# One step of a hybrid RWKV-7 / Conformer backbone on one core: a lane scheduler that stays longer in dense products, and a late modulation with stationary weights

## The chip, the core and the metric

The kernel runs on one core of a Trainium2 chip. The metric is the time of one execution on the device in microseconds (us), lower is better. Engines are named as the profile names them: PE is TensorE's products and PEld its weight loads, DVE is VectorE, ACT ScalarE, POOL GpSimd, SP the queue that issues the DMAs.

## What is computed

One trunk layer for 128 context and 512 latent tokens, D = 1024, in float32. Cut to what matters here:

```python
mod = silu(cond) @ ada_w + ada_b                      # 6 x 1024 columns: shift, scale, gate, twice
xn  = rmsnorm(x) * (1 + sc1) + sh1
rkv, glu_in, gates = split(xn @ w_in)
y_r = rwkv_branch(xn, rkv, s0_f, s0_b)                # two scans, 8 heads x 64, per-step recurrence
y_c = conv_branch(glu_in)                             # depthwise conv, LayerNorm, silu, projection
x   = x + g1 * ((sigmoid(gate_r) * y_r + sigmoid(gate_c) * y_c) @ w_o)
x   = x + g2 * (relu((rmsnorm(x) * (1 + sc2) + sh2) @ mlp_w1) ** 2 @ mlp_w2)
```

The modulation is needed in two portions: its first 16 blocks of 128 columns before the input projection, the other 32 (`for c in range(16, 48)`) only for block 1's gate, block 2 and the second norm.

## The kernel before

All activations stand feature-major: 640 tokens along the free axis in two halves of 320, 128 features on the partitions. A **dense** product is one 128x128 block of weights against 320 tokens. Each operand is split into a high and a low part in `float32r`, and three products (`mm3`) make one float32 result. Their weights come from HBM as `wr`, are split by ACT (`wh`) and DVE (`wl`), and are used in the order of `todo`. Everything else on PE is plain float32, which the trace shows as two instructions for each product: the scan's, the Gram matrices', the norms' and the late modulation's. These are called **small** products below.

The program has three stages. The first computes the early modulation, the first norm and the low-rank inputs. In the second, generators called **lanes** (`solve`, `scan`, `side`, `prep`, `lora2_all`, `ada_all`, `out_branch`, `conv_all`, `splitter`) carry the RWKV branch, the convolution and the late modulation, while `fill` supplies dense products between their steps. The third runs the output projection and the MLP, nearly all dense.

In the second stage the order of PE, DVE and ACT is fixed when the program is built, by a planner in the kernel with its own clock `now[0]` and its own costs. Each turn of the main loop calls `pick`, which returns the first lane that is due (`l[0] <= now[0]`); lanes are sorted by urgency (`URGENT`, a small number is urgent). A lane that would put products on PE (`l[1]` is None) is taken only when `hungry()` is false. Otherwise `more()` places the next dense product. `hungry()` is true while the planner believes that PE's clock has dropped, or while `credit` is below zero; each dense product raises `credit`, up to `CREDIT`, and time lowers it. What stands earlier in an engine's order is waited for: a PE product whose input is late stops all behind it.

The late modulation is the lane `ada_all`, urgency 4. For each block of 128 columns, `adl_load` fetches two halves of the weights (256 KB each) into one buffer `adl`, so that the second half's DMA can't start before the products of the first are done. `ada` then makes 2 x 4 products with the conditioning vectors `csb` stationary (32 columns) and the weights moving (128 columns), spread over four column groups of the array (`tile_position=(0, g)`). ACT copies the result out (`ade`), one product with `sel` folds the four groups, and ACT adds the bias into `mod`.

The end of the second stage: the last scan (`chain(3)`) gives `Y`; `post(3)` centres it (products `ps_t<-Y_w,cst_t`), squares it on ACT, sums it (`ps_t<-cst_t,pa_t`), takes the root on POOL, spreads it (`ps_t<-cst_t,rh_t`), multiplies on DVE by a gate loaded by DMA (`pg`), and writes the result out. `out_branch` loads it again (`ath`) and splits it; the products of the two output projections (`Side.products`, `ps_mm<-ARGH_t,...`) follow, first those of the convolution with weights in `Nb`, `Gt` and `wh`.

Of the kernel before, what the change touches and what calls it, by code (L numbers as in the profile page):

```python
# [11 lines left out]
F32R = mybir.dt.float32r  # L12
AF = mybir.ActivationFunctionType
# [4 lines left out]
P = 128  # L18
D = 1024
KD = D // P  # L20
# [33 lines left out]
NY1, NY2, NY3, CR, HG = 1, 0, 1, 1, 0  # L54
# [6 lines left out]
LEAD, SEM, LOAD = 0.40, 0.2, 4.0  # L61
BURST, REFRESH = 0, 15.0

URGENT = dict(scan=0, split=0.3, shift=1.45, post=1, side=0.9, solve=1, prep=1.5, lora=2, ada=4, out=4.5, branch=0.5, conv=1.6)

GAP_LORA, GAP_ADA = 1.5, 3.5
V_STEP = 20
GLU_AT = 12
TICK, ENTRY, QUOTA, CREDIT, DEBT = 3.413, 3060, 1.55, 200, 6000
CST_ID, CST_MASK, CST_SEL, CST_HSEL, CST_LATE = 0, 128, 256, 258, 260  # L70
NCST = 261

# [4 lines left out]
def hybrid_step(ctx: ExitStack, tc: tile.TileContext, I, O):  # L77
# [9 lines left out]
    now, free, last, ready = [0.0], dict(V=0.0, A=0.0, G=0.0), [0.0], {}  # L87
    gated = dict(cols=0.0, credit=0.0, burst=0.0, again=0.0, end=TICK, warm=True, kind=None, drain=0)
# [33 lines left out]
    V, A, G = Timed(nc.vector, "V", cost_v), Timed(nc.scalar, "A", cost_a), Timed(nc.gpsimd, "G", cost_g)  # L122

    def advance(t):
        dt, now[0] = max(t - now[0], 0.0), max(now[0], t)
        gated["credit"] = max(gated["credit"] - QUOTA * ENTRY / TICK * dt, -DEBT)
        while now[0] >= gated["end"]:
            gated.update(cols=0.0, end=gated["end"] + TICK, warm=gated["cols"] >= ENTRY)

    def bank(tag="mm"):  # L130
        return pp.tile([P, 512], F32, name="ps_" + tag, tag=tag, bufs=2 if tag == "mm" else 1)

    def st(shape, tag, bufs=1, dt=F32):
        return sb.tile(shape, dt, name=tag + "_t", tag=tag, bufs=bufs)

    def sut(shape, tag, bufs=1, dt=F32):
        return su.tile(shape, dt, name=tag + "_s", tag=tag, bufs=bufs)
# [4 lines left out]
    def ldtmp():  # L142
        pool, n, cols = tmp_pool[-1]
        return pool.tile([P, cols], F32, name="tmp", tag="tmp", bufs=n)
# [16 lines left out]
    def pc(name, i, n=1):  # L161
        return par[:, PCOL[name] + i:PCOL[name] + i + n]
# [7 lines left out]
    warm = sut([P, 512], "warm")  # L170
# [21 lines left out]
    def mm(out, lhsT, rhs, start=True, stop=True, **kw):  # L192
        PE.matmul(out=out, lhsT=lhsT, rhs=rhs, start=start, stop=stop, **kw)  # L193
        cyc = math.prod(rhs.shape[1:]) * (1 if rhs.dtype == F32R else 2 if "is_transpose" in kw else 4)
        m = math.prod(lhsT.shape[1:])
        overlap = 128 // m if m < 128 else 128 // rhs.shape[0]
        cols = cyc * rhs.shape[0] / 128 * (1 if rhs.dtype == F32R else 0.5)
        gated["cols"] += cols
        gated["burst"] -= cols
        gated["credit"] = min(gated["credit"] + cols, CREDIT)  # L200
        kind = (m, rhs.shape[0], rhs.dtype)
        if kind != gated["kind"]:
            advance(now[0] + SWITCH * gated["drain"] / (2400 if gated["warm"] else 1200))
        gated.update(kind=kind, drain=0 if rhs.dtype == F32R else max(cyc, 256) - max(cyc / overlap, 64))
        advance(now[0] + (max(cyc / overlap, 64) + EXTRA) / (2400 if gated["warm"] else 1200))
        ready[out.name] = ("P", now[0] + SEM / 2)
        last[0] = now[0]
# [167 lines left out]
    mod = st([P, 48, 2], "mod")  # L375
    csb = st([P, 2 * KD + 30], "csb")
# [6 lines left out]
    def ada(cols, tag, raws):  # L383

        n = len(cols) * P
        ps = bank(tag)
        for k0, k1, raw in raws:
            for k in range(k0, k1):
                g = 32 * (k % 4)
                mm(ps[g:g + 32, 0:n], csb[:, 2 * k:2 * k + 32], raw[:, k - k0, :], k < 4, k >= 4, tile_position=(0, g))  # L390
            yield 2.5 if k0 == 0 else 0.0
        e = ldtmp()[:, 0:n] if len(cols) > 1 else st([P, P], "ade")
        A.activation(e, ps[:, 0:n], AF.Copy)
        yield
        for i, col in enumerate(cols):
            mm(ps[:, n + 2 * i:n + 2 * i + 2], e[:, i * P:(i + 1) * P], sel)
        for i, col in enumerate(cols):
            A.activation(mod[:, col, :], ps[:, n + 2 * i:n + 2 * i + 2], AF.Identity, bias=pc("ada_b", col))
# [57 lines left out]
    ps = bank("t")  # L456
# [5 lines left out]
    for tag, a, b in (("a0", 0, 4), ("b0", 4, 5)):  # L462
        ps = bank(tag)
# [15 lines left out]
    for k in range(KD):  # L479
        run(ada((k, 8 + k), ("t", "ad")[k % 2], ada_raws[k]))  # L480
        mk_amod(0, k)
        modulate(x, k, rs, 0, SEGS, xh, xl)
        if k + AHEAD < KD:
            ada_load(k + AHEAD)
        if k == LATE:
            lora_load(1)
        if k >= SKEW:
            inner(k - SKEW)
# [66 lines left out]
    rates, operated, prepared, solved, scanned, gated_linear, added, chained, centred, grams, inverted = [set() for _ in range(11)]  # L555
# [59 lines left out]
    def adl_load(col):  # L615
        for j in range(2):
            raw = wt([P, KD // 2, P], "adl")
            DMA.dma_start(out=raw, in_=I["adal"][col - 16, :, 4 * j:4 * j + 4, :])
            yield 4 * j, 4 * j + 4, raw

    def ada_late(col):
        raws = adl_load(col)
        yield GAP_ADA
        yield from ada((col,), "ad", raws)


    smask = wt([P, T // 10], "smask")
# [515 lines left out]
    def conv_all():  # L1143
        for i in range(4):
            yield from conv(i)
        spawn(conv_branch(), URGENT["branch"])
# [147 lines left out]
    def ada_all():  # L1294
        for c in range(16, 48):
            yield from ada_late(c)
# [58 lines left out]
    def spawn(gen, urgency):  # L1355

        lanes.append([0.0, None, gen, urgency])
        lanes.sort(key=lambda l: l[3])
# [10 lines left out]
    spawn(out_branch(), URGENT["out"])  # L1369
    spawn(conv_all(), URGENT["conv"])  # L1370

    def hungry():

        return (HG == 0 or 3 not in chained) and (not gated["warm"] or gated["credit"] < 0)

    def pick(dense):

        return next((l for l in lanes if l[0] <= now[0] and (l[1] or dense)
                     and (l[1] not in free or free[l[1]] <= now[0] + LEAD)), None)

    def more():
        last[0] = now[0]
        return next(filler, False)
# [4 lines left out]
    with tc.manual_schedule(engines={ET.PE, ET.DVE, ET.Activation}):  # L1388
        while lanes:
            lane = pick(not hungry())  # L1390
            if not lane and more():
                continue
            lane = lane or pick(True)
            if lane:
                last[0] = now[0]
                try:
                    w = next(lane[2])
                    lane[0] = last[0] + SEM if w in (None, "T") else now[0] if isinstance(w, str) else now[0] + w
                    lane[1] = w if isinstance(w, str) else None
                except StopIteration:  # L1400
                    lanes.remove(lane)
            else:
                advance(min(max(l[0], free[l[1]] - LEAD if l[1] in free else 0.0) for l in lanes))
# [244 lines left out]
```

## Time and profile before

| | |
|---|---|
| median of 3 runs | 1285.7 us (1282.93 to 1289.52) |
| the profiled execution | 1274.04 us, span of its instructions 1272.3 us |
| PE busy | 1219.7 us (96% of the span), 13362 products |
| DVE / ACT / POOL busy | 739.8 (58%) / 549.7 (43%) / 28.2 us (2%) |
| mean granted clock of PE | 0.985 of full |
| the chain that ended last | PE 86%, DMA 5%, DVE 4%, issue 2%, ACT 2% |

The profiled execution is 11.7 us shorter than the median. Matmuls are pipelined, so that busy PE isn't PE at its peak: the time of a product on PE is read below from the start of one to the start of the next. The profile shows PE's clock at full speed (2.4 GHz) but for stretches at half (1.2 GHz).

### The profile page before, as it was taken

The numbers are of one execution on the slowest core, as the hardware profiler recorded it, in microseconds if no ns is written. First come the engines' busy times: TensorE is split into PE (matmuls) and PEld (weight loads), VectorE is DVE, ScalarE is ACT, GpSimd is POOL, SyncE is SP. The second block draws the span as 40 slices with busy tenths as digits, with TensorE's granted clock in tenths as the row PEclk, the third lists the DMA queues.
The fourth block names the chain that finished last, engine by engine and source line by source line (L and its number), as shares of the span: only waits on it lengthen the run. The fifth ranks groups of instructions, "written<-read, shape, count | busy, mean of one in ns | idle before, by whom it ended". The sixth has DMA issues, their size and how long they took to land.

```text
span 1272.3 us, 31723 instructions
## 1 busy us (share of the span) xinstructions
PE 1219.7 (96%) x13362; PEld 1069.1 (84%) x13362; DVE 739.8 (58%) x1606; ACT 549.7 (43%) x1390; POOL 28.2 (2%) x21
## 2 busy tenths in 40 slices
PE   8998999999999999999998999999999999999996
PEld 5776786767777777777788899999999999999996
DVE  5536587757777777587444665744433443443354
ACT  5545545644565465546552233544412431342130
POOL 0100000000000000000000000000000000000000
PEclk9999998979999999999999999999999999999998
DMA  9456443222433252233216753022222222222222
GB/s 369 157 174 184 145 120 102 83 64 67 137 97 106 86 173 93 83 118 103 74 46 186 258 195 109 26 67 83 69 81 73 77 75 76 75 75 75 75 75 83
DMA packets 82574, 140.42 MB, mean 110 GB/s; under 512 B 17024, under 2 KB 31616, under 8 KB 82432
## 3 DMA queue, kind: packets, MB, share of 16 engines
q1 hardware_dynamic: 82432, 138.39, 33.7%
q8 instruction: 105, 1.72, 0.6%
q14 instruction: 37, 0.30, 0.1%
HBM read 113.52 MB, written 22.22 MB: 107 GB/s over the span
## 4 chain that ended last, share of the span: by engine, by line
PE 86%; DMA 5%; DVE 4%; issue 2%; ACT 2%; SPq 1%; POOL 0%; POOLq 0%; DVEq 0%; ACTq 0%
PE ps_mm L193 46%; PE ps_b L193 24%; PE ps_a L193 7%; PE ps_t L193 7%; PE ps_ad L193 2%; DMA adl_w<-in_adal 2%; DMA adar_s<-in_adaw 1%; DMA z<-tmp 1%; ACT tmp L106 1%; DVE Gt_w L106 0%; DMA prod_w<-in_w 0%; DVE ARGH_t L106 0%; DVE kk_t L106 0%; DVE wl_t L106 0%; DVE vS_w L106 0%
## 5 line engine op out<-in xcount | busy, mean ns | idle before, releaser
L193 PE MATMUL ps_mm<-xh_t,wh_t 128*128 128x320 f32 x648 | 217.5, 336 | 1.8 <-ACT tmp L106 1.8
L193 PE MATMUL ps_mm<-xh_t,wl_t 128*128 128x320 f32 x648 | 213.9, 330 | 0.0
L193 PE MATMUL ps_mm<-xl_t,wh_t 128*128 128x320 f32 x648 | 213.2, 329 | 0.0
L106 ACT ACTIVATE wh_t<-wr_t 128x512 fp32r<-128x512 f32 x146 | 91.7, 628 | 134.1 <-PE ps_b L193 107.0
L106 DVE TENSOR_TENSOR wl_t<-wr_t,wh_t 128x512 fp32r<-128x512 f32 x146 | 100.2, 687 | 76.0 <-ACT wh_t L106 75.2
L193 PEld LDWEIGHTS ps_mm<-xh_t,wh_t 128*128 128x128 f32 x648 | 123.6, 191 | 21.2 <-issue 11.7
L106 ACT ACTIVATE svu_w<-ps_a 64x128 f32<-64x128 f32 x320 | 86.8, 271 | 125.3 <-PE ps_a L193 119.2
L193 PEld LDWEIGHTS ps_mm<-xl_t,wh_t 128*128 128x128 f32 x648 | 123.4, 190 | 13.7 <-issue 9.0
L193 PEld LDWEIGHTS ps_mm<-xh_t,wl_t 128*128 128x128 f32 x648 | 123.5, 191 | 9.9 <-issue 4.4
L106 DVE SCALAR_TENSOR_TENSOR cacc_w<-upad_w,par_t,cacc_w 128x640 f32<-128x640 f32 x90 | 79.2, 880 | 1.9
L193 PE MATMUL ps_mm<-ARGH_t,wh_t 128*128 128x320 f32 x268 | 72.5, 312 | 0.5 <-DVE rS_w L106 0.5
L106 ACT ACTIVATE tmp<-ps_mm 128x320 f32<-128x320 f32 x80 | 34.8, 435 | 86.8 <-PE ps_mm L193 81.7
L106 DVE TENSOR_TENSOR svu_w<-ps_b,Dc_w 64x128 f32<-64x128 f32 x152 | 43.7, 287 | 48.7 <-PE ps_b L193 45.7
L193 PE MATMUL ps_mm<-ARGH_t,wl_t 128*128 128x320 f32 x204 | 64.1, 314 | 0.4 <-DVE wl_t L106 0.4
L106 ACT ACTIVATE mwh<-wr_t 128x512 fp32r<-128x512 f32 x49 | 31.0, 633 | 72.3 <-PE ps_b L193 69.4
L106 DVE SCALAR_TENSOR_TENSOR ARGH_t<-ps_mm,mod_t,ARGH_t 128x320 f32<-128x320 f32 (+2 forms) x45 | 22.6, 512 | 59.3 <-PE ps_mm L193 59.3
L106 DVE TENSOR_TENSOR tmp<-tmp 128x320 f32<-128x320 f32 x64 | 31.1, 489 | 43.3 <-ACT tmp L106 43.2
L106 DVE TENSOR_TENSOR mwl<-wr_t,mwh 128x512 fp32r<-128x512 f32 x49 | 33.8, 690 | 36.9 <-ACT mwh L106 36.9
L193 PEld LDWEIGHTS ps_mm<-ARGH_t,wh_t 128*128 128x128 f32 x268 | 48.2, 190 | 1.3 <-issue 1.0
L106 ACT ACTIVATE BKt_w<-ps_a 32x512 f32<-32x512 f32 (+3 forms) x80 | 40.0, 502 | 17.9 <-PE ps_a L193 17.0
L193 PE MATMUL ps_mm<-xl,wh_t 128*128 128x320 f32 x140 | 43.9, 314 | 0.0
L193 PE MATMUL ps_b<-ARGH_t,wl_t 128*128 128x320 f32 x140 | 43.6, 312 | 0.0
(374 smaller groups left out, 2981.6 us busy)
## 6 DMA issues: line engine op xcount, KB each, us to landing
wr_t<-in_w SPq DMA_DIRECT2D x221, 256.0 KB, 2.7
adl_w<-in_adal SPq DMA_DIRECT2D x64, 256.0 KB, 2.8
adar_s<-in_adaw SPq DMA_DIRECT2D x16, 512.0 KB, 8.4
ARGH_t<-in_x SPq DMA_DIRECT2D x8, 640.0 KB, 6.0
z<-tmp SPq DMA_DIRECT2D x32, 160.0 KB, 2.7
gate<-tmp SPq DMA_DIRECT2D x32, 160.0 KB, 1.9
tA_t<-z SPq DMA_DIRECT2D x8, 320.0 KB, 3.5
ath_t<-z SPq DMA_DIRECT2D x8, 320.0 KB, 4.4
```

Source lines behind the costliest of these rows:

```text
L106: return f(*args, **kw)
L193: PE.matmul(out=out, lhsT=lhsT, rhs=rhs, start=start, stop=stop, **kw)
```

## The change

`hungry()` now asks for a credit of `STAY` = 350, not 0, as long as PE's last product was dense, and `CREDIT` goes from 200 to 700: once in dense products the planner stays until the credit is there, and once out of them it may stay out longer. `pick` gets patience: as long as PE's last product was dense, a lane that would put products on PE and has urgency 2 or more (late modulation, low-rank products, output branch) must have been due for 4.0 us of the planner's clock, one of 1.5 or more for 1.5, one of 1 or more for 0.6, before it ends the dense run; an urgent lane ends it at once, and then the others may go too. If no dense product can be had, patience doesn't hold. `ada_late` no longer calls `ada`: the weights are stationary (128x128), the two conditioning vectors move (2 columns), eight products add up in one bank, and one ACT instruction adds the bias. The copy, the fold with `sel` and the tile `ade` are gone.

```diff
+PATIENCE = ((2, 4.0), (1.5, 1.5), (1, 0.6))
+
-TICK, ENTRY, QUOTA, CREDIT, DEBT = 3.413, 3060, 1.55, 200, 6000
+TICK, ENTRY, QUOTA, CREDIT, STAY, DEBT = 3.413, 3060, 1.55, 700, 350, 6000
...
-        e = ldtmp()[:, 0:n] if len(cols) > 1 else st([P, P], "ade")
+        e = ldtmp()[:, 0:n]
...
     def ada_late(col):
         raws = adl_load(col)
         yield GAP_ADA
-        yield from ada((col,), "ad", raws)
+        ps = bank("ad")[:, 0:2]
+        for k0, k1, raw in raws:
+            for k in range(k0, k1):
+                mm(ps, raw[:, k - k0, :], csb[:, 2 * k:2 * k + 2], k == 0, k == KD - 1)
+                advance(now[0] + 0.08)
+            yield 2.5 if k0 == 0 else 0.0
+        A.activation(mod[:, col, :], ps, AF.Identity, bias=pc("ada_b", col))
...
+    def dense_now():
+        return gated["kind"] is not None and gated["kind"][2] == F32R
+
     def hungry():
 
-        return (HG == 0 or 3 not in chained) and (not gated["warm"] or gated["credit"] < 0)
-
-    def pick(dense):
-
+        return (HG == 0 or 3 not in chained) and (not gated["warm"] or gated["credit"] < (STAY if dense_now() else 0))
+
+    def pick(dense, patient=True):
+
+        patient = patient and dense_now()
         return next((l for l in lanes if l[0] <= now[0] and (l[1] or dense)
-                     and (l[1] not in free or free[l[1]] <= now[0] + LEAD)), None)
+                     and (l[1] not in free or free[l[1]] <= now[0] + LEAD)
+                     and (l[1] or not patient or now[0] - l[0] >= next((t for u, t in PATIENCE if l[3] >= u), 0.0))), None)
...
-            lane = lane or pick(True)
+            lane = lane or pick(True, False)
```

In PE's order the late modulation stood like this in the middle of the second stage (`ps_mm` rows are dense products, `adl_w` the weights of the late modulation, `ade_t` its copied result):

```order
L193 MATMUL ps_mm<-xh_t,wh_t 128x320
L193 MATMUL ps_ad<-adl_w,csb_t 32x128 x4
L193 MATMUL ps_mm<-xl_t,wh_t 128x320
L193 MATMUL ps_mm<-xh_t,wl_t 128x320
L193 MATMUL ps_mm<-xh_t,wh_t 128x320
L193 MATMUL ps_mm<-xl_t,wh_t 128x320
L193 MATMUL ps_mm<-xh_t,wl_t 128x320
L193 MATMUL ps_mm<-xh_t,wh_t 128x320
L193 MATMUL ps_ad<-cst_t,ade_t 128x2
```

The change, at a block of columns in the middle of the second stage (`ps_a`, `ps_b` and `ps_t` with `svu_w` are the two half-steps of a scan and their output):

```order
L195 MATMUL ps_b_2409<-svu_w,BKt_w 64x64 x4
L195 MATMUL ps_a_2408<-cst_t,vS_w 32x64 x2
L195 MATMUL ps_a_2408<-cst_t,vr_w 32x64 x2
L195 MATMUL ps_ad<-csb_t,adl_w 128x2 x4
L195 MATMUL ps_mm<-xh_t,wh_t 128x320
L195 MATMUL ps_mm<-xl_t,wh_t 128x320
L195 MATMUL ps_mm<-xh_t,wl_t 128x320
```

Four products of the late modulation now follow a scan's half-step at once instead of standing alone between dense ones, and the fold is gone. In the whole program the 5712 dense products stand in 381 runs before and in 237 now.

PE's order before at the end of the last scan, from its last output to the centring of `Y`, with dense products (`Gt_w` holds weights here) between:

```order
L193 MATMUL ps_t<-ARGH_t,svu_w 64x32 x4
L193 MATMUL ps_mm<-xl_t,Gt_w 128x320
L193 MATMUL ps_mm<-xh_t,Gt_w 128x320 x2
L193 MATMUL ps_mm<-xl_t,Gt_w 128x320
L193 MATMUL ps_mm<-xh_t,Gt_w 128x320 x2
L193 MATMUL ps_mm<-xl_t,Gt_w 128x320
L193 MATMUL ps_t<-Y_w,cst_t 64x320 x2
```

The change, through the last one and a half steps of the last scan and `post(3)` to the first products of the convolution's projection (`Nb_w` holds their weights):

```order
L195 MATMUL ps_a_7971<-svu_w,ARGH_t 32x64 x4
L195 MATMUL ps_t<-ARGH_t,svu_w 64x32 x4
L195 MATMUL ps_b_7972<-svu_w,BKt_w 64x64 x4
L195 MATMUL ps_a_7971<-cst_t,vS_w 32x64 x2
L195 MATMUL ps_a_7971<-cst_t,vr_w 32x64 x2
L195 MATMUL ps_a_7971<-svu_w,ARGH_t 32x64 x4
L195 MATMUL ps_t<-ARGH_t,svu_w 64x32 x8
L195 MATMUL ps_t<-Y_w,cst_t 64x320 x4
L195 MATMUL ps_t<-cst_t,pa_t 128x2 x5
L195 MATMUL ps_t<-cst_t,rh_t 64x128 x10
L195 MATMUL ps_mm<-ARGH_t,Nb_w 128x320 x24
```

No dense product is left between: the last one but the 384 of the two output projections stands one step further up, two and a half steps before the scan's end. Before, dense products stood in every gap, and 60 that are not of the projections still came behind `ps_t<-cst_t,rh_t`.

## Rows read from the trace of the kernel before

**Rows 1.** Windows: us; busy of PE, PEld, DVE, ACT, POOL; clock; DMA; GB/s.
```profile
62.00:680.00 618.00, 588.88 (x9083) 459.14 (x9082) 420.18 (x953) 330.74 (x954) 18.83 (x10) 0.98 0.35 109
680.00:745.00 65.00, 58.95 (x386) 56.62 (x387) 39.27 (x77) 17.94 (x34) 0.00 (x0) 1.00 0.78 252
745.00:1272.30 527.30, 514.38 (x3504) 513.36 (x3503) 244.74 (x495) 169.05 (x330) 3.40 (x4) 0.99 0.24 76
```

**Rows 2.** The chain that ended last, third stage: start us, us, what.
```profile
1083.19 3.52 PE ps_mm L193 x24
```

**Rows 3.** Timeline of PE from 138 us: start us, us, operation, count.
```profile
138.05 0.31 PE L193 MATMUL ps_mm<-xh_t,wl_t 128*128 128x320 f32 x1
138.29 0.43 PE L193 MATMUL ps_ad<-adl_w,csb_t 128*32 128x128 f32 x8
138.65 0.42 PE L193 MATMUL ps_mm<-xh_t,wh_t 128*128 128x320 f32 x1
138.90 0.31 PE L193 MATMUL ps_mm<-xl_t,wh_t 128*128 128x320 f32 x1
...
140.30 0.28 PE L193 MATMUL ps_ad<-cst_t,ade_t 128*128 128x2 f32 x2
140.44 0.39 PE L193 MATMUL ps_mm<-xh_t,wl_t 128*128 128x320 f32 x1
140.67 0.31 PE L193 MATMUL ps_mm<-xh_t,wh_t 128*128 128x320 f32 x1
```

**Rows 4.** Waits of PE, 62 to 685 us: us in total, times, longest.
```profile
PE ps_ad L193 <- DMA adl_w<-in_adal: 8.8, 7, 2.7
PE ps_t L193 <- DVE kk_t L106: 6.5, 5, 3.1
```

**Rows 5.** Windows around half-clock stretches, columns as in rows 1.
```profile
200.30:207.20 6.90, 6.39 (x29) 4.22 (x29) 3.95 (x10) 2.09 (x5) 0.00 (x0) 0.51 0.50 171
...
272.00:289.10 17.10, 16.89 (x180) 12.69 (x180) 7.50 (x20) 5.98 (x19) 0.00 (x0) 0.50 0.15 47
289.10:306.20 17.10, 17.10 (x225) 12.45 (x222) 13.77 (x45) 8.42 (x20) 0.00 (x0) 1.00 0.20 63
620.20:623.60 3.40, 3.40 (x39) 3.05 (x39) 1.30 (x5) 0.11 (x1) 0.85 (x1) 1.00 0.23 76
623.60:627.00 3.40, 3.40 (x26) 2.83 (x26) 0.93 (x2) 2.08 (x8) 0.00 (x0) 0.50 0.17 41
```

**Rows 6.** Groups by form: count, busy us, mean ns, idle before.
```profile
L193 PE MATMUL ps_ad<-adl_w,csb_t 128*32 128x128 f32 x512 | 27.7, 289 | 8.9 <-DMA adl_w<-in_adal 8.8
```

**Rows 7.** Timeline of PE: a group with 128x128 stationary and 2 columns moving.
```profile
664.02 1.17 PE L193 MATMUL ps_t<-cst_t,pa_t 128*128 128x2 f32 x10
665.06 0.39 PE L193 MATMUL ps_mm<-xl_t,wh_t 128*128 128x320 f32 x1
```

**Rows 8.** Timeline of PE: one scan step, from first half to first half.
```profile
595.64 0.32 PE L193 MATMUL ps_a<-svu_w,ARGH_t 128*32 128x64 f32 x8
...
598.47 0.32 PE L193 MATMUL ps_a<-svu_w,ARGH_t 128*32 128x64 f32 x8
```

**Rows 9.** Timeline of PE from the last scan's end to the output projections.
```profile
657.85 0.42 PE L193 MATMUL ps_t<-ARGH_t,svu_w 128*64 128x32 f32 x8
...
659.42 0.76 PE L193 MATMUL ps_t<-Y_w,cst_t 128*64 128x320 f32 x4
...
670.33 0.41 PE L193 MATMUL ps_mm<-xh_t,wl_t 128*128 128x320 f32 x1
...
682.73 3.49 PE L193 MATMUL ps_mm<-ARGH_t,Nb_w 128*128 128x320 f32 x22 [1.53 <-DVE Nb_w L106]
```

**Rows 10.** Timeline of DVE in the same place.
```profile
676.56 0.83 DVE L106 TENSOR_TENSOR vS_w<-vS_w,pg_t 128x640 f32<-128x640 f32 x1 [3.36 <-DMA pg_t<-g]
677.31 0.82 DVE L106 TENSOR_TENSOR ARGH_t<-ath_t,ARGH_t 128x640 fp32r<-128x640 f32 x1
...
681.99 0.68 DVE L106 TENSOR_TENSOR Nb_w<-prod_w,Nb_w 128x512 fp32r<-128x512 f32 x1
```

## The prediction

> **What bounds the kernel now.** I read the windows by stage first. The third stage is PE alone: 514.4 of 527.3 us busy [rows 1]. The chain shows there what a dense product costs when others follow it: 24 in 3.52 us, so 0.147 us each [rows 2]. The change doesn't reach this stage. In the second stage PE is busy for 588.9 of 618 us, DVE for 420 and ACT for 331 [rows 1]: PE sets the end, and its time goes into some 1700 dense products, 9083 instructions in all, the moves between dense and small ones, waits, and half clock. So the prices of those four have to be read one by one.
>
> The price of a move stands in the timeline [rows 3]. From the last dense product to the first small one it is 138.05 to 138.29, 0.24 us; from the first dense one behind them to the next, 138.65 to 138.90, 0.25 us. In a run both would be 0.147. **A round trip costs 0.19 us** beyond the products' own time. It isn't paid by every small group: around the fold (128x128 stationary) the dense product before starts 0.147 us ahead, and only the 0.23 us behind it is long.
>
> The waits of PE on the late modulation's DMA are 8.8 us in seven, the longest 2.7; of those on DVE's `kk` the longest is 3.1 [rows 4]. The windows show the third loss: PE's clock was at half for 6.9, 17.1 and 3.4 us [rows 5]. The first two begin at the end of such waits (on `kk`, on `adl`). The third is another kind: in the 3.40 us ahead of it PE was busy all the time, mostly with a norm's sums, whose products move one column.
>
> What half clock costs: 180 PE instructions in the 17.1 us against 225 in the next 17.1 [rows 5], 20%; by the ratio of the two levels it would be 50%. I take 35% of the stretch: 2.4 us for one of 6.9, and 9.6 us for the 27.4.
>
> **The change, part by part.** *Late modulation.* A column was two groups of eight instructions (512 in all over 32 columns [rows 6]) and a fold. A group is 138.05 to 138.90, 0.85, less two dense spacings and the 0.19: 0.37 us. The fold is 0.14 and 0.08 of the longer spacing behind it, 0.22 [rows 3]. Sum 0.96. Now it is sixteen instructions with 128x128 stationary and two columns moving. The trace has this form: the group of ten from 664.02 to 665.06 [rows 7], and 0.08 behind it as for the fold, so 1.12 us for ten, 0.112 each, and no round trip. Sixteen are 1.79 us. **Term: (1.79 - 0.96) x 32 = +26.5 us.** Nothing hides it: it is PE's own time. The Trainium skill, "TensorE: Matmul & The Clock Gate", section "Back-to-back issue gap", gives up to 64 moving columns a spacing of about 25 ns; by that, 512 instructions would be an estimated 12.8 us and this term about -18. Rows 7 contradict it for this form at full clock, with a new weight load for each product, so the row decides.
>
> *Longer dense runs.* In the order, 364 groups of small products stand between dense runs of the second stage before and 220 after; those that hold a product on part of the array, and so pay the round trip, are 328 and 207. Runs of three dense products or fewer drop from 185 to 17. **Term: 121 x 0.19 = -23.0 us.** That the planner does what the change says is thus not in doubt.
>
> *Waits.* The second half's DMA can start only behind the first half's products. With the durations of the rows, twelve groups of the late modulation stood less than 4.2 us behind the one before; now the closest are 5.2 us apart, because the lane must have been due for 4 us. **Term: -8.8 us**, bounds 0 and -8.8: SP can still be held by another DMA, but the new room is larger than the longest of these waits. Of the 3.1 us on `kk`, which is a chain of DVE work and may stay, I take half, -1.6 us (0 to -3.1).
>
> *Clock.* The two stretches behind waits go with the waits: 24.0 us at 35%, -8.4 us. Against this, small products now stand together for longer. By the durations of the rows, groups of 3 us and more between two dense products are 4 before and 16 after (two of them about 6 us). One of the 4 was followed by half clock. The Trainium skill, "TensorE: Matmul & The Clock Gate", section "Why this matters for your kernels", names idle gaps as what loses the clock; by that these groups would cost nothing, since PE works through them. Rows 5 have the clock falling behind 3.40 busy us of 3.40, so I count them: a quarter of the 16, 4 stretches of 6.9 us, 9.6 us less the 1.2 of the one before. **Term: +8.4 us**, bounds 0 and +18 (half of them). The two clock terms cancel.
>
> *The end of the second stage.* Lanes advance less for each dense product, so the dense ones run out two and a half scan steps before the last scan ends. What the path there takes without filler: two steps of 2.83 us, the shortest step of the trace [rows 8], 1.4 for the last half-step, 0.9 to the centring; from there to the end of the spreading 10.9 us in the trace [rows 9] with dense products between, of which I take 10, since the links (DVE, ACT, the root on POOL, PE's own groups) follow each other anyway. Then 670.33 to the weights `Nb`: the DMA of `pg` ended at 676.56, DVE multiplies, splits `ath` and splits `Nb`, 0.83 + 0.82 + 0.68 [rows 10]: 8.5 us. All this is queued in DVE's order ahead of the first projection's weights, and nothing else is left for PE. Sum 26.5 us, in which PE has 7.8 us of small products: **18.7 us idle**. Before, the same place held 62 dense products (9.1 us) in the 12.4 us from 670.33 to 682.73 [rows 9], so 3.3 us idle. Difference +15.4, and one stretch of half clock as in the 6.9 us window, +2.4. **Term: +17.8 us**, bounds +5 (the links overlap and the clock holds) and +25 (a cold start of the projections as long as the 17.1 us stretch).
>
> ACT loses 32 copies and some 9 us of work; it wasn't waited for in that lane, so nothing. The third stage and the first don't change.
>
> **Sum:** 26.5 - 23.0 - 8.8 - 1.6 - 8.4 + 8.4 + 17.8 = +10.9 us. The terms come from the profiled execution, 1274.0 us, which would become 1284.9. It lies 11.7 us under the median of the runs shown; taking that distance as the same for both, the time is 1285.7 + 10.9 = **1297 us**.
>
> **The rivals.** *Same: the end costs less.* If the chain behind the last dense product is mostly hidden, at the lower bound of +5, the sum is -2 and the time 1284. For it speaks that the links are short; against it, that PE's order there holds no dense product at all.
>
> *Faster: the late modulation slips under the rest.* If the weight loads of the new products ran beside other work, and they started 0.046 us apart as the old ones did (0.37 by eight), a column would be 0.74 us, the term -7.0 and not +26.5, the time 1263. It decides from a spacing of 0.078 us down, where the sum passes -6.4. The trace has the form itself at 0.112, which leaves this little. The section of the Trainium skill on the issue gap, cited above, would bring it about too.
>
> *Faster or same: the clock.* The median is 11.7 us over the profiled execution. If that is half clock behind DMA waits that this execution happened to miss, the change takes it away, and the time is 1285; if the long groups of small products cost nothing as well, 1277. For it: two of three stretches here began behind waits. Against: I have one execution.
>
> *Slower still: the small groups.* If half of the 16 groups lose the clock, +18 in place of +8.4, and the end at its upper bound, the sum is +28 and the time about 1311.
>
> **How the numbers follow.** My forecast, 1290 to 1305 us, has 0.43; slower still 0.14; the two cases that end near 1285 together 0.27; the clock with free small groups 0.11; the late modulation hidden 0.05. The bound of 0.5%, 6.4 us, is about what a measurement of this kernel can tell from no change. So slower has 0.57, the same 0.27, faster 0.16. The range leaves out about one in ten on each side: 1278 to 1311.
>
> **What would show it.** Right: the late modulation's products 0.11 us apart and some 57 us of PE in all; fewer round trips, with dense runs of four and more; no DMA wait on `adl` worth naming; PE idle for 15 us or more between the last scan's end and the first product with `Nb`; half-clock windows behind long groups of small products. Wrong: the products closer than 0.08 us, PE busy through the end of the stage, or a mean clock above 0.985.

## The result, and the profile after

The changed kernel takes 1303.0 us in the median of five runs (1298.9 to 1306.4), the kernel before 1285.7 in five beside them. The ratio is 1.0133, 95% interval 1.0091 to 1.0174: slower, by 17.3 us. The forecast was 1297, range 1278 to 1311. Some executions of a kernel fall into a second, slower state of the chip; medians, ratios and mean clocks here are those of the others. The profiled execution takes 1301.0 us with a span of 1299.1, the one of before 1274.0. So the two profiles lie 27.0 us apart, the medians 17.3; that difference comes back below.

The windows by stage, first the lanes up to the last scan's end, then from there to the projections' products, then the third stage (columns as in [rows 1]):

```profile
62.00:685.00 623.00, 600.10 (x8993) 508.68 (x8992) 414.44 (x936) 320.27 (x916) 16.41 (x9) 0.95 0.35 108
685.00:705.80 20.80, 8.88 (x47) 5.48 (x45) 9.05 (x21) 7.27 (x15) 2.13 (x1) 0.50 0.18 59
...
752.00:1299.10 547.10, 533.64 (x3624) 532.02 (x3624) 254.70 (x516) 171.89 (x336) 3.40 (x4) 0.99 0.26 84
```

The third stage is the same, as forecast: from the projections' second group of products (686.06 us before, 711.85 now) to the end of the span it is 586.2 us before and 587.2 now. What is new stands before it: the lanes reach their end at 685 us where it was 658 [rows 9], the clock there is 0.95 and not 0.98 [rows 1], and then PE works 8.88 of 20.80 us, all of it at half clock.

The late modulation, the row of all its products and one group in the timeline, with the scan's product ahead and the dense one behind:

```profile
L195 PE MATMUL ps_ad<-csb_t,adl_w 128*128 128x2 f32 x512 | 69.5, 258 | 0.5 <-DMA adl_w<-in_adal 0.5
```

```profile
233.54 0.32 PE L195 MATMUL ps_a<-svu_w,ARGH_t 128*32 128x64 f32 x8
233.79 1.05 PE L195 MATMUL ps_ad<-csb_t,adl_w 128*128 128x2 f32 x8
234.71 0.39 PE L195 MATMUL ps_mm<-xh_t,wl_t 128*128 128x320 f32 x1
```

Eight instructions from 233.79 to 234.71, 0.115 us each; summed over the trace, from the start of each to the start of the next, the 512 take 60.5 us, 0.118 each. The forecast had 0.112 from [rows 7], and 57.3.

The waits of PE, 62 to 720 us (total, times, longest):

```profile
PE ps_t L195 <- DVE vS_w L108: 8.3, 9, 2.1
PE ps_t L195 <- DVE kk_t L108: 7.6, 10, 1.3
PE ps_mm L195 <- DVE Nb_w L108: 6.1, 1, 6.1
...
PE ps_ad L195 <- DMA adl_w<-in_adal: 0.5, 1, 0.5
```

The wait on the late modulation's DMA is gone, 8.8 us to 0.5 [rows 4]. That on `kk` isn't, and the same kind on `vS`, 5.3 us in five before, has grown to 8.3.

The half clock, in windows of 3.40 us that end where it begins, and one of it:

```profile
408.10:411.50 3.40, 2.25 (x39) 1.64 (x36) 2.79 (x9) 1.83 (x8) 0.00 (x0) 1.00 0.22 80
575.40:578.80 3.40, 1.32 (x20) 0.91 (x16) 2.86 (x4) 0.14 (x1) 0.00 (x0) 0.99 0.44 124
640.20:643.60 3.40, 3.40 (x36) 3.26 (x35) 1.30 (x5) 0.44 (x2) 0.00 (x0) 1.00 0.03 12
...
411.50:421.70 10.20, 10.20 (x75) 8.40 (x74) 5.14 (x18) 4.99 (x14) 0.00 (x0) 0.50 0.13 44
```

Eight stretches begin in the lanes, all in or just behind a group of small products that keeps two dense ones 3 us or more apart. By the traces there are 26 such groups in the lanes where before has 9; the forecast had 16 and 4, and a quarter that lose the clock. Ahead of six stretches PE was also idle, for 0.7 to 2.1 us of the 3.40 (the first two rows); ahead of the other two it was busy throughout (the third). The last of the eight begins at 667.5 us and lasts to 711.9, through the whole end of the stage. The lanes have 62 us of half clock where the profile of before has 27. The Trainium skill, "TensorE: Matmul & The Clock Gate", section "Why this matters for your kernels", names idle gaps as the cause. Idle time, though never for the whole 3.40 us, stands ahead of six of the eight; ahead of the other two there is none.

Those two come behind the same work, the sums of a norm, 24 instructions in a row that move one column each; the first and the last:

```profile
640.65 0.28 PE L195 MATMUL ps_t<-ones_t,u_t 128*128 128x1 f32 x2
...
643.02 0.36 PE L195 MATMUL ps_t<-ones_t,tB_t 128*128 128x1 f32 x2
```

The profiles of all runs have 22 such groups that begin at full clock. During 21 of them, or within 2 us behind, a half-clock stretch begins; in the 3.40 us ahead of it PE was busy throughout in 15 cases and idle for at most 0.54 us in the others. The one group that kept the clock is the second of the kernel before. So these groups, which stand in both kernels, lose the clock nearly every time. No run changes them, so that it is their doing, and by what, is not shown.

The end of the second stage, PE and then DVE:

```profile
676.25 0.63 PE L195 MATMUL ps_mm<-xh_t,Gf_w 128*128 128x320 f32 x1
...
684.65 0.77 PE L195 MATMUL ps_t<-ARGH_t,svu_w 128*64 128x32 f32 x8 [0.48 <-DVE Y_w L108]
...
690.51 2.29 PE L195 MATMUL ps_t<-cst_t,pa_t 128*128 128x2 f32 x10 [1.36 <-ACT pa_t L108]
695.35 1.97 PE L195 MATMUL ps_t<-cst_t,rh_t 128*64 128x128 f32 x16 [2.54 <-POOL rh_t L108]
...
705.82 6.22 PE L195 MATMUL ps_mm<-ARGH_t,Nb_w 128*128 128x320 f32 x22 [6.12 <-DVE Nb_w L108]
711.85 3.71 PE L195 MATMUL ps_mm<-ARGH_t,Gt_w 128*128 128x320 f32 x24
```

```profile
703.60 0.82 DVE L108 TENSOR_TENSOR vS_w<-vS_w,pg_t 128x640 f32<-128x640 f32 x1 [3.14 <-DMA pg_t<-g]
704.34 0.82 DVE L108 TENSOR_TENSOR ARGH_t<-ath_t,ARGH_t 128x640 fp32r<-128x640 f32 x1
705.08 0.68 DVE L108 TENSOR_TENSOR Nb_w<-wr_t,Nb_w 128x512 fp32r<-128x512 f32 x1
```

It is the chain of the forecast, link by link: the last dense product, the steps, centring, squares (on ACT), the root on POOL, the DMA of `pg`, three pieces of work on DVE, `Nb`. It takes 29.6 us (676.25 to 705.82) where 26.5 were forecast. The first 22 products of the projections then take 6.03 us at half clock, where 22 times 0.147 is 3.2.

### The profile page after: what moved, and what is told of

Its sections match the earlier page's. It is cut to its first block, busy times and chain, and to the rows that moved or that the text cites. A ratio compares the mean times of both kernels' runs of the same rounds, so it can differ in the third digit from the quotient of the medians.

```text
span 1299.1 us, 31576 instructions
## 1 busy us (share of the span) xinstructions
PE 1242.7 (96%) x13298; PEld 1128.9 (87%) x13298; DVE 741.9 (57%) x1606; ACT 541.8 (42%) x1358; POOL 27.9 (2%) x21
## 4 chain that ended last, share of the span: by engine, by line
PE 79%; DVE 3%; issue 2%; ACT 1%; DMA 1%; POOL 0%; SPq 0%; POOLq 0%; DVEq 0%; ACTq 0%
PE ps_mm L195 40%; PE ps_b L195 23%; PE ps_t L195 6%; PE ps_a L195 6%; PE ps_ad L195 4%; DVE vS_w L108 1%; DVE ARGH_t L108 1%; DMA u_t<-gate 0%; DVE kk_t L108 0%; DVE wl_t L108 0%; ACT BKt_w L108 0%; DMA adl_w<-in_adal 0%; ACT svu_w L108 0%; DMA pg_t<-g 0%; DVE u_t L108 0%
## 5 line engine op out<-in xcount | busy, mean ns | idle before, releaser
L195 PE MATMUL ps_mm<-xh_t,wh_t 128*128 128x320 f32 x672 | 221.3, 329 | 0.3 <-ACT tmp L108 0.3
L195 PE MATMUL ps_mm<-xl_t,wh_t 128*128 128x320 f32 x672 | 219.1, 326 | 0.0
L195 PE MATMUL ps_mm<-xh_t,wl_t 128*128 128x320 f32 x672 | 217.8, 324 | 0.0
L108 ACT ACTIVATE wh_t<-wr_t 128x512 fp32r<-128x512 f32 x150 | 94.3, 629 | 141.4 <-PE ps_b L195 107.3
L108 DVE TENSOR_TENSOR wl_t<-wr_t,wh_t 128x512 fp32r<-128x512 f32 x150 | 103.0, 687 | 76.6 <-ACT wh_t L108 74.4
L195 PEld LDWEIGHTS ps_mm<-xh_t,wh_t 128*128 128x128 f32 x672 | 130.1, 194 | 5.8 <-issue 1.4
L195 PEld LDWEIGHTS ps_mm<-xl_t,wh_t 128*128 128x128 f32 x672 | 130.1, 194 | 4.9 <-issue 1.7
L195 PEld LDWEIGHTS ps_mm<-xh_t,wl_t 128*128 128x128 f32 x672 | 129.8, 193 | 5.1 <-issue 2.5
L195 PEld LDWEIGHTS ps_ad<-csb_t,adl_w 128*128 128x128 f32 x512 | 65.4, 199 | 6.2 <-issue 1.8
L195 PE MATMUL ps_ad<-csb_t,adl_w 128*128 128x2 f32 x512 | 69.5, 258 | 0.5 <-DMA adl_w<-in_adal 0.5
```

Of the source, the lines that this page charges most:

```text
L108: return f(*args, **kw)
```

## Two halves of the change by themselves

**The late modulation alone**, under the old rules:

```diff
-        yield from ada((col,), "ad", raws)
+        ps = bank("ad")[:, 0:2]
...
+                mm(ps, raw[:, k - k0, :], csb[:, 2 * k:2 * k + 2], k == 0, k == KD - 1)
```

> The kernel before with one part of the change alone: the late modulation with its weights stationary, the old rules for lanes. The theory of the prediction: 512 products at 0.112 us against 0.96 us a column, +26.5 us, less 40 round trips that go with the old form (328 to 288, 0.19 us each, -7.6): 1300 to 1306 us, 1.1 to 1.6% slower. The waits on the late modulation's DMA stay, 5 to 10 us. Rival, the new products slip under other work: 1275 to 1285 us, not slower.

1304.6 us, ratio 1.0156 (1.0092 to 1.0221): +20 us, and the rival falls. The new products take 0.111 us from start to start, summed over the trace. The waits on their DMA stay:

```profile
PE ps_ad L193 <- DMA adl_w<-in_adal: 6.1, 7, 2.1
```

**The rules alone**, with the old form of the products:

```diff
-        ps = bank("ad")[:, 0:2]
-        for k0, k1, raw in raws:
...
+        yield from ada((col,), "ad", raws)
```

> The changed kernel with the late modulation in its old form: the new rules for lanes alone. The theory of the prediction: round trips -23 us, waits -10, the clock near 0, the end of the stage +10 to +18: 1268 to 1280 us, so 0.5 to 1.4% faster than before and some 26 us under the changed kernel. Rival, the loss lies in the new rules (long groups of small products at half clock and an empty end of the stage) and the form of the products is worth little: 1290 to 1303 us.

1268.9 us, ratio 0.9881 (0.9836 to 0.9926): 15 us faster than before. The forecast's own sum without its +26.5 is -15.6. This is the lowest time of the study, though in the profiled execution (1280.4 us, the slowest of its seven) the end is longer than that of the changed kernel (PE's wait, and the window from the last scan's last product to `Nb`):

```profile
PE ps_mm L195 <- ACT Nb_w L108: 14.7, 1, 14.7
```

```profile
651.70:686.70 35.00, 16.98 (x95) 12.83 (x93) 14.66 (x33) 13.18 (x31) 3.01 (x2) 0.50 0.22 72
```

## Is it the two moving columns?

The products of the late modulation move 2 columns; the order stays as it is, and each moves 32:

```diff
-        ps = bank("ad")[:, 0:2]
+        ps = bank("ad")[:, 0:32]
...
-                mm(ps, raw[:, k - k0, :], csb[:, 2 * k:2 * k + 2], k == 0, k == KD - 1)
+                mm(ps, raw[:, k - k0, :], csb[:, 2 * k:2 * k + 32], k == 0, k == KD - 1, like=csb[:, 0:2])
```

(`like` keeps the planner's price.)

> The changed kernel, its order of instructions unchanged, but each product of the late modulation moves 32 columns instead of 2 (30 of the results are not read). Theory A, the clock falls in stretches where PE is busy with products that move few columns: the spacing stays near 0.118 us, the mean granted clock rises from 0.958 to 0.965 or more, the time falls by 5 to 9 us to 1294 to 1298. Theory B, the clock falls for another reason (waits, the end of the stage) and these products are not it: clock 0.956 to 0.962 and 1300 to 1306 us. If the 30 columns more make the products longer (0.03 us for each of 512), both come out 15 us higher.

1302.3 us, ratio 1.0134 (1.0081 to 1.0186), mean clock 0.9585 over its runs where the changed kernel has 0.9584. Theory B: neither the time nor the clock hangs on whether these products move 2 columns or 32.

```profile
L195 PE MATMUL ps_ad<-csb_t,adl_w 128*128 128x32 f32 x512 | 70.6, 283 | 0.4 <-DMA adl_w<-in_adal 0.4
```

Start to start they take 60.0 us, against 60.5 with 2 columns. That up to 64 columns cost the same is also what the Trainium skill says, "TensorE: Matmul & The Clock Gate", section "Back-to-back issue gap"; but its spacing is some 25 ns, and here it is 117. What a product costs in this form is paid for 2 columns as for 32.

## The rules one by one

**Without patience** (`PATIENCE = ()`), everything else as changed:

> The changed kernel without patience: every lane that is due may end a dense run, once the credit is there. In the order 217 round trips in place of 207, runs of one to three dense products 53 in place of 18, and at the end dense products stand again between the last steps. The theory of the prediction: +2 for the round trips, 3 to 9 us of waits on the late modulation's DMA come back, and the end of the stage gives 10 to 18 back: 1290 to 1302 us. Rival, patience is what brings the half clock (it lets small groups pile up): 1280 to 1290 us and half clock of under 20 us ahead of the end.

1314.3 us, ratio 1.0246 (1.0194 to 1.0298), outside all that was expected. The profiled execution is far from that median, 1338.6 us at a mean clock of 0.943, so only its waits are shown:

```profile
PE ps_mm L195 <- ACT wh_t L108: 15.6, 1, 15.6
PE ps_ad L195 <- DMA adl_w<-in_adal: 12.1, 9, 4.7
```

The waits on `adl` are back, so patience has its part in removing them; in the profile of the rules alone, with patience and the old form, 4.4 us in five are left. That these waits make up the 11 us over the changed kernel is not shown. The mean clock is 0.957 to 0.963 in the executions behind the median, and 0.956 to 0.962 in the changed kernel: the half clock is about the same without patience, and the rival falls.

**Patience alone**, in the old form of the products, with `STAY` 0 and `CREDIT` 200:

```diff
-TICK, ENTRY, QUOTA, CREDIT, STAY, DEBT = 3.413, 3060, 1.55, 700, 350, 6000
+TICK, ENTRY, QUOTA, CREDIT, STAY, DEBT = 3.413, 3060, 1.55, 200, 0, 6000
```

> The late modulation in its old form, patience as in the change, but STAY 0 and CREDIT 200 as before: patience alone. 205 round trips where both rules give 207 and the kernel before has 328. If patience carries the gain of the new rules, 1265 to 1273 us, as with both. If staying in dense products carries it, 1278 to 1286 us.

1325.7 us, ratio 1.0322 (1.0271 to 1.0374), outside both expectations, 57 us over both rules together, with as few round trips (205 against 207). The windows tell why:

```profile
554.20:652.10 97.90, 81.08 (x1680) 60.84 (x1678) 64.23 (x152) 47.53 (x157) 1.95 (x1) 0.60 0.20 63
...
663.70:725.80 62.10, 48.66 (x539) 35.98 (x537) 23.84 (x74) 33.83 (x108) 3.65 (x3) 0.55 0.09 29
```

In these 160 us no dense product starts, but for one of the projections at their end. The planner places one whenever no lane is due, so by its rules it had none left that could be used yet; the lanes go on alone, mostly at half clock. Fewer moves between dense and small products are no gain by themselves.

**The planner's price.** It counts a product of the late modulation at 0.107 us (0.027 and the 0.08 of the diff), where the two instructions of a product take 0.236:

```diff
-                advance(now[0] + 0.08)
+                advance(now[0] + 0.19)
```

> The changed kernel with one number of its planner changed: a product of the late modulation counts 0.217 us on the planner's clock (0.19 in place of 0.08 added to 0.027), near the 0.236 that it takes in the profile (two instructions of 0.118), where it counts 0.107. In the order 182 round trips in place of 207. Theory P, since the planner thinks that these products take half their time, it lets small groups pile up and believes the clock up when it is down: with the true price the mean granted clock rises from 0.958 to 0.966 or more, and with 5 us of round trips the time falls to 1286 to 1294 us. Rival, the half clock has nothing to do with the planner's price: clock 0.955 to 0.962, 1296 to 1302 us. Third, fewer groups are longer groups, and the dense products run out earlier: clock under 0.955, over 1302.

1320.8 us, ratio 1.0268 (1.0222 to 1.0314), mean clock 0.951: the third case. Fewer round trips once more (182), and in the profile (the second slowest of six) the lanes at 0.92; and the last dense product ahead of the projections stands at 680.9, 26 us ahead of the last scan's last product (4.7 and 8.8 us ahead with the old form and in the changed kernel; before, they reach 21 us past it):

```profile
62.00:706.90 644.90, 610.50 (x8995) 520.27 (x8993) 411.66 (x928) 319.97 (x911) 16.20 (x9) 0.92 0.33 104
680.90:732.50 51.60, 28.99 (x255) 22.51 (x253) 20.30 (x56) 22.34 (x58) 3.04 (x2) 0.51 0.15 52
```

## Filling the end

Dense products that nobody reads are added where PE has nothing else, first with a bank taken anew for each:

```diff
+                if late_done and 2 in chained:
...
+                    mm(bank("ad")[:, 0:H2], xl[:, 0, 0:P], xh[:, 0, 0:H2])
+                    yield True
```

> The changed kernel with 147 dense products more, whose result nobody reads, in the places where PE has nothing else at the end of the second stage; the order of all other products up to the last scan's end is the same. Were PE's idle time there filled without use, as if only the length of the chain of DVE, ACT and POOL counted, the time stays at 1303 (1300 to 1306) us, though PE has 21.6 us more to do. If the half clock (44 us in the profile, through the whole end) makes the chain's own small products and the first dense ones longer, the full clock gives back 4 to 10 us: 1293 to 1299. If the added products push the chain back, it is longer than 1306.

1396.2 us, ratio 1.0858 (1.0789 to 1.0927). The run tests something else than meant: 160 such products took 0.66 us each from start to start and pushed everything back; each takes its bank anew, and with one bank, below, they take 0.16.

```profile
692.52 4.79 PE L195 MATMUL ps_ad<-xh_t,xl_t 128*128 128x320 f32 x7
```

The same with one bank, taken once, and from a slightly earlier point on:

> As in the earlier run with 147 added dense products at the end of the second stage, but all of them go to one bank that is taken once, so that none waits for another: 0.147 us each at full clock, 21.6 us in all. If the half clock of the end (44 us in the profile of the changed kernel) lengthens the chain, the clock stays up and the time is 1293 to 1299 us, the mean clock 0.968 or more. If only the length of the chain counts, 1300 to 1306. If the added products push the chain back, as they did at 0.617 us each, over 1306.

1308.3 us, ratio 1.0189 (1.0135 to 1.0244); mean clock 0.970. Not faster. From the last scan's last product to the wait's end it is 19.1 us where it was 20.8, and the 22 products behind it take 4.6 us, not 6.0:

```profile
689.00:708.10 19.10, 12.90 (x101) 10.74 (x97) 8.08 (x19) 7.00 (x14) 2.14 (x1) 0.90 0.17 53
```

```profile
708.15 4.78 PE L195 MATMUL ps_mm<-ARGH_t,Nb_w 128*128 128x320 f32 x22 [4.81 <-DVE Nb_w L108]
712.77 3.69 PE L195 MATMUL ps_mm<-ARGH_t,Gt_w 128*128 128x320 f32 x24
...
729.79 4.71 PE L195 MATMUL ps_a<-xh_t,xl_t 128*128 128x320 f32 x31
```

So 3.1 us came back at the end, not 4 to 10; the chain counts. It isn't all that full clock could give there: the clock is 0.90 in the window, and at half again for those 22 products, which at 0.147 would take 3.2 us. The added products cost more than that elsewhere: 75 of the 160 fell behind 712.77, among the products of the projections and after (31 of them in the last row), and from there to the end it is 8.3 us longer than in the changed kernel.

On the rules alone:

> The new rules for lanes with the late modulation in its old form, and the same added dense products at the end of the second stage. Without them 1269 us at a clock of 0.970, with 41 us of half clock at the end. If the end's half clock costs there what it does elsewhere (about 0.37 us for each us), 8 to 15 us come back: 1254 to 1262 us. If the chain alone counts: 1266 to 1272.

1278.1 us, ratio 0.9938 (0.9903 to 0.9973), clock 0.979: outside both expectations, and 7 us (by the ratios) over the same kernel without them, which has 0.970. A mean clock raised in this way is no gain.

## Filling the waits on `kk` and `vS`

The two halves of a sum or a norm use one bank, and PE stands while DVE reads it. A step ends there now:

```diff
-            if NY3 and h == 0:
-                yield 0.0
+            if h == 0:
+                yield
...
             bc(P * a, P * b, pb[:, 0:P * (b - a)])
+            if a == 0:
+                yield
```

> The changed kernel with a step of the lane ended between the two halves of a sum or a norm, where PE's next product needs the one bank that DVE is still reading (19 waits on kk and vS, 15.9 us in the profile). PE now has another product there; 202 round trips where there were 207. Theory W, the half clock of the lane stage begins at these waits: they go (10 to 14 us) and the half clock ahead of the end falls from 62 us to under 35, 10 us more: 1278 to 1288 us. Theory T, it comes from long groups of small products, busy or not: only the waits go, the half clock stays: 1288 to 1296. Theory F, dense products are a fixed stock, and those that fill the gaps are missing at the last scan's end: 1298 to 1306.

1296.1 us, ratio 1.0082 (1.0052 to 1.0112). The waits:

```profile
PE ps_t L195 <- DVE vS_w L108: 2.3, 3, 0.8
...
PE ps_t L195 <- DVE kk_t L108: 1.7, 3, 0.9
```

15.9 us became 4.0. But the mean clock over its runs is 0.960 where it was 0.958: theory W falls for this kernel, though six of eight stretches began behind idle time. The time is that of theory T's upper edge: a little over half of the 12 us of waits shows in it, and where the rest goes is not shown.

> The new rules for lanes, the late modulation in its old form, and the same ends of steps: a version that may beat both. Without them 1269 us, with 14.0 us of such waits in 18. Theory W 1245 to 1255 us, theory T 1255 to 1262, theory F 1266 to 1272.

1277.2 us, ratio 0.9916 (0.9881 to 0.9950): no gain on the rules alone (0.9881), and slower than all three theories had it. A wait of 13.3 us on `wh` stands at the end, as one of 14.7 on `Nb` did there; so the reason is not shown.

> The kernel before with the same ends of steps alone. Its waits on kk and vS are 11.8 us in ten, the half clock ahead of the last scan's end 27 us in the profile. Theory W 1266 to 1274 us, theory T 1274 to 1280, theory F 1283 to 1289; 329 round trips where there were 328.

1273.3 us, ratio 0.9915 (0.9875 to 0.9955): 11 us faster than before, with a mean clock of 0.978 against 0.972. The waits on `kk` and `vS` fall from 11.8 to 2.0 us, and the time by about as much. It lies in the range of theory W, at the edge to T, and the clock rose; so for the kernel before it stays open whether the waits brought some of its half clock. Under the new rules the same edit bought less or nothing.

## Why the prediction was right, and where it was off

The side and the time came as forecast. Term by term, on the two profiles:

- **Late modulation**, +26.5: 60.5 us now against 30.7 (0.96 x 32), +29.8, a part of it at half clock (29 of the 512 took 6.2 us). Alone it cost +20 on the kernel before, where 40 round trips went with it (-7.6): +27.6. Right. That it slips under other work is refuted.
- **Round trips**, -23.0: from 62 us to the last scan's last output (657.85 before, 684.65 now), from each start to the next and without waits, the dense products at full clock took 66.2 us more than 0.147 each before (1572 products) and 38.7 now (1621): -27.5. Right, somewhat too small.
- **Waits**, -8.8 and -1.6: `adl` -8.3, right. `kk` +1.1 instead of -1.6, and `vS`, not looked at, +3.0. The step that took half of the longest `kk` wait as gone was wrong: small products stand behind small ones now, and nothing dense fills the time while DVE still works on what they read.
- **The end**, +17.8: in PE's order, 107 dense products besides those of the projections stood there before (15.7 us), none now. From 684.65 to 705.82 it is 21.2 us, 3.7 less than from 657.85 to 682.73 [rows 9], and the 22 products behind it take 2.8 more: +14.8. Right, somewhat too large. PE idles 11.9 us there, where the sign of being right asked for 15; from the last dense product (676.25) it is 14.0 us, where 18.7 were forecast, since the small products, at half clock, take 14.0 us and not 7.8.
- **Clock**, -8.4 and +8.4: on the profiles wrong. The lanes have 35 us more of half clock, not the same. Of the long groups about the expected share lost the clock (8 of 26, a quarter was forecast), but there are 26 of them and not 16; and stretches behind idle time, which were to go, are six and not none.

Without the clock these sum to +12.9 (forecast: 10.9). The remaining 14.1 us of the profiles' 27.0 are about what those 35 us cost, at the price that follows.

What a us of half clock costs can be read from executions of one kernel, since each has its mean clock: 60 of the kernel before go from 1275.7 us at 0.982 to 1297.4 at 0.962, 10.3 us for 0.01 in a line through all. As 0.01 of mean clock is 25.7 us of half clock, that is 0.40 us for each; the forecast took 0.35.

The same executions show why the medians lie only 17.3 us apart. Their mean clock is 0.972, and the profiled one, at 0.985, had some 33 us less of half clock than the usual, 13 us by that price: that covers its 11.7 us under the median. The changed kernel's executions lie at 0.956 to 0.962, the profiled at 0.958 and 1.9 us under the median. So the step that took the distance as the same for both was wrong, and so was the clock term on the profiles, and they are one error in two places: a lucky profile. In the usual execution before has 71 us of half clock and the changed kernel 108, of which 27 stand at the end, where the added products won back some 3. The rest is 10 us more, 4 us of time: by this estimate a clock term near zero, as forecast. No profile shows where a usual execution of before has its half clock, so it stays an estimate; and that the two errors cancel in the median, where 1297 came near 1303, is luck. The rival that explained the median by half clock was right in that and wrong in that the change would take it away.

That the parts add to +5 (+20 and -15) and the change to +17 isn't fully settled; the intervals are 5 to 8 us to either side. The clock is lower with both parts (0.958) than with either (0.971, 0.970), and the lanes' half clock in the profiles goes the same way (62 us; 40 and 35). By the line above, 0.012 of clock are 12 us, as much as is missing. Put otherwise, the new products cost 34 us on the new rules (1268.9 to 1303.0) and 20 on the old ones; the forecast had one price for both, and put the added half clock down to the rules alone. What makes it lower was not found: not whether the late modulation moves 2 columns or 32, not the waits on `kk` and `vS`, not the planner's price.

## What to carry to other kernels

A few columns are better moved past stationary weights only if a product's cost goes with its columns: look first for a product of that form in the trace. Filler is a stock: a rule that uses more of it for each step of a dependent chain leaves the end of the chain bare, and counting the filler behind its last link in the order is as needful as counting the moves saved. Before a sum is made against one profiled execution, its mean clock is to be compared with that of others.

## Unexpected on the chip

An fp32 instruction with 128x128 weights takes as long with 32 moving columns as with 2: 0.117 and 0.118 us. In or just behind 21 of 22 groups of 24 instructions that move one column PE's clock fell to half, though PE was busy or nearly so. Dense products that each waited for the one before (0.67 us apart) did not bring the clock back: PE counted as busy for 76.83 of 85.30 us, all at half clock.

```profile
678.50:763.80 85.30, 76.83 (x282) 42.54 (x279) 18.66 (x48) 15.89 (x41) 2.13 (x1) 0.50 0.09 29
```
